# The tile of x1 serves once as a page for weights, then collects the experts' sums; x1 is added from its two parts later

## The chip, the cores and the metric

The kernel runs on 1 core of a Trainium2 chip. The metric is device time in microseconds (us) of one execution. Five engines work beside each other: PE (TensorE, matrix products; its weight loads are shown as PEld), DVE (VectorE), ACT (ScalarE), POOL (GpSimd) and SP (SyncE), which here does nothing but issue DMA transfers, in the order of the program. SBUF is the on-chip memory (128 partitions), PSUM the eight banks of 128 x 512 f32 into which PE writes.

## What is computed

One layer of an encoder on 256 tokens of width 2048, in f32. The part that matters here, cut from the reference:

```python
    x = x + merged @ w_out[i]                      # x1
    x = x + _hier_moe(_rmsnorm(x, g_ffn[i]), ...)  # 32 experts, top 2 of one group
    gate_p = jax.nn.sigmoid(_rmsnorm(x, g_ple[i]) @ w_ple_gate[i] + b_ple_gate[i])
    x = x + gate_p * (p[i] @ w_ple_up[i])
return _rmsnorm(x, g_final)
...
        hid = jax.nn.silu(xb @ w_g[e]) * (xb @ w_u[e])
        return (hid @ w_d[e]) * wt[:, None].astype(xb.dtype)
```

Ahead of it stand two token mixers with dense projections. An expert has w_gate and w_up of 2048 x 512 and w_down of 512 x 2048, 12 MB in f32; all 32 are read.

## The kernel before, in words

**Tokens and layout.** The 256 tokens are two blocks b of 128 partitions. `X[b]` is 128 x 2048 f32 (8 KB a partition) and holds x; `evac_out` adds the output projection into it chunk by chunk (four chunks c of 512 columns, L673), which makes x1. From there on X is called X2 and collects the experts' results.

**Pages and the stream.** All large weights come as pages of 128 x 4096 f32 (2 MB), each in one DMA (two of 1 MB for some). Class `Stream` (L40 on) holds a list `todo` of the loads in the order in which they will be used, and a list of free pages. `add(page)` tells that a page has been read; `pump` then issues the next load of the list into it (L67). Since SP works in the order of the program, an issue that must wait for the readers of its page also holds up every issue behind it. `add_half` (L74) and `add` (L82) issue a page in two halves at the first pair of experts.

The ring of pages in the expert stage has four pages `page`, two `pageX` and two `pageR` (called passing), eight in all; two are taken out on the way (`KEEP`: one from pair 4 on, which becomes `hpage`, and one from pair 8 on, for a product of the last part), so that six are left. The tile `pagePT` holds the tokens sorted for the experts (`xT`) and joins the ring after the loop.

**Two parts.** f32 products that matter for accuracy are made from two fp32r parts, hi and lo, whose sum is the f32 number. `evac_out`'s `lay` lays x1 as such parts `XP[b]` with columns rearranged ("t (p k) -> t k p", a step of 16 numbers, 64 bytes): hi is a copy by ACT (L680), lo = x1 − hi is a subtraction by DVE (L684). For the last chunk, lo is subtracted by POOL (L682, the list `last_lo`), beside the routing.

**Routing.** After x1 is ready PE makes the router's logits (L714 to L724), then warm-up transposes `keep_warm` (L300, 38 of them, then 20) while DVE works through a chain of small operations (L766 to L807) that finds each token's two experts; PE waits for its result at L811. Then one-hot matrices are made (L874, L876) and `dispatch` (L887, L890) sorts tokens by products with `XP`.

**The loop over pairs of experts** (P = 0 to 15; i = 0 gate, 1 up; j = four quarters of the rows; two quarters share a page of each of two experts):
- `gate_up` (L909): f32 products, two experts side by side on PE's columns, 16 per quarter.
- `hidden_gate` (ACT, L916), `hidden_up` (DVE, L920), `hidden_t` (PE transposes L924, ACT copy L925).
- in the next pair: `down_early(P-1)` (L974), the split of its result into hi and lo (`split_y`: ACT L933, DVE L934), and `combine_early(P-1)` (L963), which brings rows back to tokens, with a DVE addition into X2 (L967).
- for P below 8 w_down takes four pages; from P = 8 on only a first part of 512 columns is done in the loop, one page, and the remaining columns come in the tail.
- in odd pairs `dispatch` sorts tokens for the next two. After P = 6 there is a branch for experts with more than 64 tokens (`tc.If`, L984/L985), which SP waits for too.

The loads stand in the list in this order for each pair: gate quarters 0 and 1 (two pages, one per expert), w_down of the pair before, gate quarters 2 and 3, up 0 and 1, up 2 and 3. At the end come w_down of pair 15, then the remaining columns of w_down of pairs 8 to 10 (one page each, called i0, i1, i2), one page of `w_ple_gate`, i3, i4 and so on.

At P = 15 `st.retiring = True` takes both `pageR` out of the ring as they come free: their pool `rt2`, which holds `XP` too, is released after the loop, and the tail's tiles (`fin`, with the accumulators `ACC`) lie there.

**The tail** does the remaining products of w_down (L974), combines them (L1117, `add_rows` into X2), makes the gated term with three fp32r products (L1138 to L1140) and the final norm.

```python
 78      def add(self, *pages):
...
 85              if passing and self.retiring:
 86                  continue
```

Of the kernel before, what the change touches and what calls it, by code (L numbers as in the profile page):

```python
# [7 lines left out]
F32 = mybir.dt.float32  # L8
# [15 lines left out]
NL = NP - FULL  # L24
PPLE = 9
WARM = 12, 4
ROUTE_WARM = 38, 20
PARTS = ([(i, 2 * h + j) for h in range(2) for i in range(2) for j in range(2)],
         [(i, j) for i in range(2) for j in range(4)])
KEEP = {(4, 0, 1): 1, (8, 0, 1): 1}  # L30
# [9 lines left out]
class Stream:  # L40


    def __init__(self, nc):
        self.nc = nc
        self.free = deque()
        self.todo = deque()
        self.ready = deque()
        self.wanted = 0
        self.kept = deque()
        self.passing = []  # L50
        self.second = []
        self.retiring = False

    def want(self, *parts):

# [22 lines left out]
    def add(self, *pages):  # L78

        for page in pages:  # L80
            if self.second and page is self.second[0][0]:
                self.nc.sync.dma_start(page[:, 2048:4096], self.second.pop(0)[1][:, 2048:4096])  # L82
                continue
            passing = any(page is q for q in self.passing)
            if passing and self.retiring:
                continue
            if self.wanted and not passing:
                self.wanted -= 1
                self.kept.append(page)
            else:  # L90
                self.free.append(page)
        self.pump()
# [46 lines left out]
def body(tc, x, p, g_mix, w_in, w_pool, pool_scale, w_branch_a, sgu_ln_g, sgu_ln_b, w_spatial,  # L139
# [14 lines left out]
    psum = tc.alloc_tile_pool(name="psum", bufs=1, space=bass.MemoryType.PSUM)  # L154
    PS = [psum.tile([128, 512], F32, name=f"ps{i}") for i in range(8)]
    cst = tc.alloc_tile_pool(name="cst", bufs=1, side="left")
    cst.tile([128, 8], F32, name="gap0")
    base = tc.alloc_tile_pool(name="base", bufs=1, side="left")
    X = [base.tile([128, 2048], F32, name=f"x{b}") for b in range(2)]
    pg_pt = base.tile([128, 4096], F32, name="pagePT")  # L160
    pages = [base.tile([128, 4096], F32, name=f"page{i}") for i in range(4)]
    pg_pm, pg_t = pg_pt[:, 0:2048], pg_pt[:, 2048:4096]
# [438 lines left out]
                                       op=OP.mult)  # L601


    more = None
    MT, XP, yh, yl = [], [], [], []
    SG = [[pg_t[:, (2 * i + b) * 512:(2 * i + b + 1) * 512] for b in range(2)] for i in range(2)]

# [25 lines left out]
    for c in range(4):  # L633
        for i in range(2):
            unit(hT, evac_gate(c, i))
        if c == 0:
            drain()
            wk.release()
            mg = tc.alloc_tile_pool(name="mg", bufs=1, side="left", reuse_waits="tile")
            MT.extend(mg.tile([128, 512], F32R, name=f"mT{k}") for k in range(16))  # L640
            st.add(pages[3])
        if c == 1:
            bg.append(wr_gain)
        unit(zT, evac_y(c, 0))
        if c == 3:
            last_y = evac_y(c, 1)

            def end_y(banks):
                nonlocal rt, more
                todo = last_y(banks)  # L650
                rt.release()
                more = tc.alloc_tile_pool(name="more", bufs=1, side="right", reuse_waits="tile")
                rt = tc.alloc_tile_pool(name="rt2", bufs=1, side="right", reuse_waits="tile")
                st.passing = [rt.tile([128, 4096], F32, name=f"pageR{i}") for i in range(2)]
                XP.extend([rt.tile([128, 2048], F32R, name=f"x{n}{i}") for n in "hl"] for i in range(2))
                yh.extend(more.tile([128, 512], F32R, name=f"yh{i}") for i in range(2))
                yl.extend(more.tile([128, 512], F32R, name=f"yl{i}") for i in range(2))
                st.add(*st.passing)
                return todo

            unit(gT, end_y)
        else:
            unit(gT, evac_y(c, 1))
# [5 lines left out]
    def evac_out(c):  # L669
# [6 lines left out]
        def lay(b):  # L676

            hi, lo = (t.rearrange("t (k p) -> t k p", k=16)[:, :, 32 * c:32 * c + 32] for t in XP[b])
            src = X[b][:, cs].rearrange("t (p k) -> t k p", k=16)
            S_.activation(hi, src, AF.Copy)  # L680
            if c == 3:
                last_lo.append(lambda: P_.tensor_tensor(lo, src, hi.bitcast(F32), op=OP.subtract))  # L682
            else:
                V_.tensor_tensor(lo, src, hi.bitcast(F32), op=OP.subtract)  # L684

# [67 lines left out]
    oce = [ex.tile([128, T], F32R, name=f"oce{i}") for i in range(2)]  # L753
    hTe = [ex.tile([128, 4, 128], F32, name=f"hTe{i}") for i in range(2)]
    st.add(*[ex.tile([128, 4096], F32, name=f"pageX{i}") for i in range(2)])
    iot = ex.tile([128, 4, CAP], F32, name="iot")
    P_.iota(iot, pattern=[[WIN, 4], [1, CAP]], base=0, channel_multiplier=0, allow_small_or_imprecise_dtypes=True)
    rw = [hid[:, i * 64:(i + 1) * 64].rearrange("p (a e) -> p a e", a=8) for i in range(6)]
    ms1 = sm("ms1", [128, 2])
    vsum(ms1, ss1)  # L760
    r1 = inv_rms(ms1, "r1")
    for f in last_lo:
        f()
    L = sm("L", [128, 2, 36])
    for b in range(2):
        V_.scalar_tensor_tensor(L[:, b, :], lg[:, b, :], r1[:, b:b + 1], rb,  # L766
# [1 line left out]
    dbg("x1", X)  # L768
    dbg("L", [L])

    keep_warm(ROUTE_WARM[0], PS[4])

    Lg = L[:, :, 0:4]
# [184 lines left out]
    def combine_early(P, h):  # L958
        for c in ((2 * h, 2 * h + 1) if P < FULL else (0,) if not h else ()):
            banks = YE[0:2] if c % 2 else (T0, T1)  # L960
            for b in range(2):
                for y in (yh, yl):
                    mm(banks[b], oce[P % 2][:, b * 128:b * 128 + 128], y[c % 2], start=(y is yh), stop=(y is yl),  # L963
                       skip_group_check=True)
            for b in range(2):
                cs = slice(c * 512, (c + 1) * 512)
                V_.tensor_tensor(X2[b][:, cs], X2[b][:, cs], banks[b], op=OP.add)  # L967
        if not h and P < FULL:
            for c in range(2, 4):
                split_y(c % 2, YE[c], 512)  # L970
# [52 lines left out]
    def p_up():  # L1023
# [14 lines left out]
                S_.activation(pp[b][:, n * 512:(n + 1) * 512], (C0, C1)[b], AF.Copy)  # L1038
        st.add(page)

    onehots(lambda i, b: SW[:, i, b:b + 1])
    dispatch(xT, 0)
    dispatch(xT, 1)
# [3 lines left out]
    for P in range(NP):  # L1047
# [4 lines left out]
            pp = [page[:, b * D:(b + 1) * D] for b in range(2)]  # L1052
            p_up()
        if P == NP - 1:
            st.retiring = True
        for i, j in PARTS[bool(P)]:
            acc = accs[i]
            if not j % 2:
# [16 lines left out]
            if P == 0:  # L1075
                if (i, j) in ((0, 1), (1, 0)):
                    dispatch(xT, 2 + i)
                if (i, j) == (1, 1):
                    ci = late_routing()
            elif P % 2 and P < NP - 1 and i:  # L1080
                if j == 0:
                    onehots(lambda i, b: SQ[:, i, b, P // 2 + 1:P // 2 + 2])
                dispatch(xT, j)
            if (i, j) == (0, 2):
                slot_weights(pid[:, P:P + 1], wsl[:, P:P + 1])
                slot_scales(pid[:, P:P + 1], rsl[:, P:P + 1])
# [10 lines left out]
    down_early(NP - 1)  # L1097


    rt.release()  # L1100
    fin = tc.alloc_tile_pool(name="fin", bufs=1, side="right", reuse_waits="tile")
    oc2 = [fin.tile([128, 2 * T], F32R, name=f"oc{i}") for i in range(NL // 2)]
    oc = [oc2[i // 2][:, i % 2 * T:(i % 2 + 1) * T] for i in range(NL)]
    lx = [fin.tile([128, 512], F32R, name=f"lx{i}") for i in range(4)]
    flow = Flow(nc, fin, bg, look=2)
    gxs = [[fin.tile([128, 512], F32R, name=f"gx{i}{k}") for k in range(4)] for i in range(2)]
    gx, gx_idle = gxs[1], gxs[0]
    st.add(pg_pt)
    S_.activation(wsl[:, 0:1], wsl[:, 0:1], AF.Sigmoid)
    ACC = [fin.tile([128, 2048], F32, name=f"acc{b}") for b in range(2)]  # L1110
    ss2, ss3 = sm("ss2", [128, 2, 5]), ss0
    SPANS = ((0, EC),) + CHUNKS

# [212 lines left out]
```

## Time and profile before

| | us |
|---|---|
| median of 3 runs (1621.5 to 1624.71) | 1623.43 |
| the profiled execution | 1622.31 |
| its span in the profile | 1620.5 |

The granted TensorE clock is 0.979 in the mean. Busy time and share of the span:

| engine | us | share |
|---|---|---|
| PE | 1519.7 | 94% |
| PE weight loads | 879.0 | 54% |
| DVE | 633.8 | 39% |
| ACT | 422.6 | 26% |
| POOL | 26.6 | 2% |

DMA moves 526.64 MB, 325 GB/s in the mean. The expert stage runs from about 552 us (first L887) to about 1384 us, the tail from there.

In a timeline each row is start, duration, engine, line, operation, out<-in and the number of instructions that the row groups; in square brackets stands how long the engine was idle before it and what ended that. Rows with `SPq` are the issuing of DMA transfers by SP: a long one is a group with waits inside. A row of stretches has start:end, length, busy time and number of instructions of PE, PEld, DVE, ACT and POOL, then the granted clock, the mean busy share of the 16 DMA engines, and GB/s. A row of grouped instructions has busy time in us and the mean in ns of one, then the idle time before them and what ended it.

### The profile page before, as it was taken

What the parts mean: (1) busy time and instruction counts of PE and PEld (TensorE: products, weight loads), DVE (VectorE), ACT (ScalarE), POOL (GpSimd) and SP (SyncE); (2) the same over time, 40 slices, a digit from 0 to 9 for tenths busy, and PEclk for the clock granted to TensorE, in tenths of its full rate; (3) what the DMA queues carried; (4) which work ended last, traced back from release to release, by engine and by line L of the source; (5) the groups of instructions that cost most, each with busy time, mean ns of one, the idle gap of its engine ahead of it and who ended that gap; (6) DMA issues with size and microseconds to landing.
All of it is one profiled execution on the core that took longest, in us unless ns stands there. A gap on an engine that the chain in (4) does not pass through costs nothing. (4 is left out here: it accounts for less than half of the span.)

```text
span 1620.5 us, 17459 instructions
## 1 busy us (share of the span) xinstructions
PE 1519.7 (94%) x7009; PEld 879.0 (54%) x7009; DVE 633.8 (39%) x1119; ACT 422.6 (26%) x746; POOL 26.6 (2%) x38
## 2 busy tenths in 40 slices
PE   8999999999999999989979879999897987999994
PEld 6788888888888734324324324334242422456663
DVE  5764565656566414204213203212120211333457
ACT  4644454454455210100000000010000000332234
POOL 0000000000000100000000000000000000000004
PEclk9999999999999999999999989999999998999997
DMA  9656675555564699999999999999999999999881
GB/s 331 222 162 162 210 238 184 191 188 184 194 248 175 248 382 427 429 427 426 427 427 426 427 383 427 425 422 421 422 421 422 422 422 369 391 365 314 280 304 53
DMA packets 133096, 526.64 MB, mean 325 GB/s; under 512 B 16720, under 2 KB 43664, under 8 KB 110992
## 3 DMA queue, kind: packets, MB, share of 16 engines
q1 hardware_dynamic: 119184, 520.12, 82.1%
q10 hardware_dynamic: 13824, 5.34, 1.3%
q8 instruction: 57, 0.93, 0.2%
q14 instruction: 31, 0.25, 0.0%
HBM read 523.33 MB, written 2.10 MB: 324 GB/s over the span
## 5 line engine op out<-in xcount | busy, mean ns | idle before, releaser
L909 PE MATMUL ps<-page,pagePT 128*64 128x512 f32 x912 | 339.9, 609 | 11.9 <-DMA page<-in_w_exp_gate_dram 8.6
L121 DVE TENSOR_TENSOR wlo<-page,whi 128x512 fp32r<-128x512 f32 x358 | 246.6, 692 | 195.2 <-ACT whi L120 189.7
L120 ACT ACTIVATE whi<-page 128x512 fp32r<-128x512 f32 x358 | 224.7, 631 | 240.3 <-PE ps L394 207.1
L909 PE MATMUL ps<-pageX,pagePT 128*64 128x512 f32 x576 | 208.8, 622 | 24.3 <-DMA pageX<-in_w_exp_gate_dram 13.1
L909 PE MATMUL ps<-pageR,pagePT 128*64 128x512 f32 x560 | 189.3, 617 | 17.1 <-DMA pageR<-in_w_exp_gate_dram 10.8
L392 PE MATMUL ps<-whi,hT 128*128 128x512 f32 x448 | 184.3, 411 | 1.5 <-ACT whi L120 1.5
L934 DVE TENSOR_TENSOR yl<-ps,yh 128x512 fp32r<-128x512 f32 (+2 forms) x72 | 44.7, 630 | 344.8 <-ACT yh L933 344.8
L393 PE MATMUL ps<-wlo,hT 128*128 128x512 f32 x448 | 178.9, 399 | 0.4 <-DVE wlo L121 0.4
L394 PE MATMUL ps<-whi,hT 128*128 128x512 f32 x448 | 178.5, 399 | 0.0
L909 PEld LDWEIGHTS ps<-page,pagePT 128*64 128x64 f32 x912 | 96.9, 139 | 148.3 <-issue 125.5
L933 ACT ACTIVATE yh<-ps 128x512 fp32r<-128x512 f32 (+2 forms) x72 | 39.6, 549 | 361.6 <-PE ps L974 293.2
L909 PEld LDWEIGHTS ps<-pageX,pagePT 128*64 128x64 f32 x576 | 62.7, 142 | 113.8 <-issue 76.5
L909 PEld LDWEIGHTS ps<-pageR,pagePT 128*64 128x64 f32 x560 | 54.4, 141 | 84.2 <-issue 65.1
L392 PEld LDWEIGHTS ps<-whi,hT 128*128 128x128 f32 x448 | 85.2, 190 | 20.4 <-ACT whi L120 2.0
L394 PEld LDWEIGHTS ps<-whi,hT 128*128 128x128 f32 x448 | 85.0, 190 | 20.6
L393 PEld LDWEIGHTS ps<-wlo,hT 128*128 128x128 f32 x448 | 85.3, 190 | 19.4 <-DVE wlo L121 1.0
L890 DVE TENSOR_TENSOR pagePT<-ps,gfp 128x512 f32<-128x512 f32 x64 | 44.3, 692 | 130.8 <-PE ps L887 130.8
L967 DVE TENSOR_TENSOR x<-x,ps 128x512 f32<-128x512 f32 x80 | 50.0, 683 | 99.3 <-PE ps L963 99.3
L920 DVE SCALAR_TENSOR_TENSOR hid<-hid,wsl,ps 128x512 f32<-128x512 f32 x16 | 17.6, 1103 | 150.0 <-PE ps L909 149.2
L887 PE MATMUL ps<-OHd,xh 128*128 128x256 f32 x256 | 65.7, 295 | 0.0
L974 PE MATMUL ps<-page,hTe 128*64 128x512 f32 x224 | 59.8, 610 | 2.7 <-DMA page<-in_w_exp_down_dram 2.7
L887 PE MATMUL ps<-OHd,xl 128*128 128x256 f32 x256 | 62.1, 280 | 0.0
(271 smaller groups left out, 1842.9 us busy)
## 6 DMA issues: line engine op xcount, KB each, us to landing
page<-in_w_exp_gate_dram SPq DMA_DIRECT2D x32, 2048.0 KB, 19.8
page<-in_w_exp_up_dram SPq DMA_DIRECT2D x23, 2048.0 KB, 21.4
pageX<-in_w_exp_up_dram SPq DMA_DIRECT2D x21, 2048.0 KB, 20.0
pageR<-in_w_exp_up_dram SPq DMA_DIRECT2D x20, 2048.0 KB, 21.0
page<-in_w_merge_gate_dram SPq DMA_DIRECT2D x32, 1024.0 KB, 5.7
pageX<-in_w_exp_gate_dram SPq DMA_DIRECT2D x15, 2048.0 KB, 18.2
pageR<-in_w_exp_gate_dram SPq DMA_DIRECT2D x15, 2048.0 KB, 21.1
page<-in_w_exp_down_dram SPq DMA_DIRECT2D x14, 2048.0 KB, 23.6
```

Source lines behind the costliest of these rows:

```text
L120: nc.scalar.activation(hi, src, AF.Copy)
L121: nc.vector.tensor_tensor(lo, src, hi.bitcast(F32), op=OP.subtract)
L392: mm(banks[b], ah, hi, start=(k == 0), stop=False, skip_group_check=True)
L393: mm(banks[b], ah, lo, start=False, stop=False, skip_group_check=True)
L394: mm(banks[b], al, hi, start=False, stop=(k == nk - 1), skip_group_check=True)
L887: mm(ps[:, kk, :], XP[b][part][:, at:at + 128], OHd[:, b, 0:n], start=(not b and not part), stop=bool(b and part), skip_group_check=True)
L890: V_.tensor_tensor(xT[j][:, 2 * h:2 * h + 2, 0:n], ps, gfp[:, k0:k0 + 2, None].to_broadcast([128, 2, n]), op=OP.mult)
L909: mm(acc[i * 64:i * 64 + 64, :], xT[k // 4][:, k % 4, at + i * CAP:at + (i + 1) * CAP], ws[i], start=(k == 0), stop=(k == 15), skip_group_ ...
L933: S_.activation(yh[i][:, 0:w], y[:, 0:w], AF.Copy)
L934: V_.tensor_tensor(yl[i][:, 0:w], y[:, 0:w], yh[i][:, 0:w].bitcast(F32), op=OP.subtract)
L967: V_.tensor_tensor(X2[b][:, cs], X2[b][:, cs], banks[b], op=OP.add)
L974: mm(y[i * 64:i * 64 + 64, :], ht[:, k, i * 64:i * 64 + 64], ws[i], start=(k == 0), stop=(k == 3), skip_group_check=True)
```

## The change

1. X[0] and X[1] become the halves of one tile `pageS`, as large as a page. When x1's parts are laid, `pageS` is given to the stream for one load (`st.once`: a page in this list is not refilled). It takes the ninth load of the expert stage, the first gate page of P = 1. Then X2 lies in it: the first sums (of P = 0) are copied there by ACT instead of being added by DVE, and at P = 14 `add_x1` adds x1's hi and lo, sixteen DVE additions of 128 x 512, at a step of 64 bytes in X2.
2. The lo part of the last chunk is made by PE instead of POOL: identity x x1 (f32) plus negated identity x hi (fp32r) into PSUM, and a copy by ACT. The first warm-up has 20 transposes instead of 38. DVE makes the negated identity `nident` ahead of the routing chain.
3. `retiring` goes. At P = 15 only the first `pageR` leaves the ring; the second stays until the end of the loop, and holds `ACC` in the tail. `XP` gets a pool of its own, which the tail's other tiles take over.
4. `gap0` grows from 8 to 32 columns, which shifts the left side's tiles by 96 bytes.

```diff
-ROUTE_WARM = 38, 20
+ROUTE_WARM = 20, 20
...
         self.passing = []
+        self.once = []
         self.second = []
-        self.retiring = False
...
+            if any(page is q for q in self.once):
+                continue
             passing = any(page is q for q in self.passing)
-            if passing and self.retiring:
-                continue
...
-    cst.tile([128, 8], F32, name="gap0")
+    cst.tile([128, 32], F32, name="gap0")
     base = tc.alloc_tile_pool(name="base", bufs=1, side="left")
-    X = [base.tile([128, 2048], F32, name=f"x{b}") for b in range(2)]
+    pg_x = base.tile([128, 4096], F32, name="pageS")
+    X = [pg_x[:, b * 2048:(b + 1) * 2048] for b in range(2)]
...
                 more = tc.alloc_tile_pool(name="more", bufs=1, side="right", reuse_waits="tile")
+                xp = tc.alloc_tile_pool(name="xp", bufs=1, side="right", reuse_waits="tile")
                 rt = tc.alloc_tile_pool(name="rt2", bufs=1, side="right", reuse_waits="tile")
-                st.passing = [rt.tile([128, 4096], F32, name=f"pageR{i}") for i in range(2)]
-                XP.extend([rt.tile([128, 2048], F32R, name=f"x{n}{i}") for n in "hl"] for i in range(2))
+                XP.extend([xp.tile([128, 2048], F32R, name=f"x{n}{i}") for n in "hl"] for i in range(2))
+                st.passing = [(rt, more)[i].tile([128, 4096], F32, name=f"pageR{i}") for i in range(2)]
...
             if c == 3:
-                last_lo.append(lambda: P_.tensor_tensor(lo, src, hi.bitcast(F32), op=OP.subtract))
+                last_lo.append((b, lo, hi))
...
+    nident = ex.tile([128, 128], F32R, name="nident")
...
-    for f in last_lo:
-        f()
...
+    V_.tensor_scalar(nident, ident, -1.0, None, op0=OP.mult)
+    for b, lo, hi in last_lo:
+        ps = PS[3 + 2 * b].rearrange("t (k p) -> t k p", k=16)
+        mm(ps, ident, X[b][:, 1536:2048].rearrange("t (p k) -> t k p", k=16), start=True, stop=False, skip_group_check=True)
+        mm(ps, nident, hi, start=False, stop=True, skip_group_check=True)
+        S_.activation(lo, ps, AF.Copy)
+    st.add(pg_x)
+    st.once.append(pg_x)
     keep_warm(ROUTE_WARM[0], PS[4])
...
-                V_.tensor_tensor(X2[b][:, cs], X2[b][:, cs], banks[b], op=OP.add)
+                if P:
+                    V_.tensor_tensor(X2[b][:, cs], X2[b][:, cs], banks[b], op=OP.add)
+                else:
+                    S_.activation(X2[b][:, cs], banks[b], AF.Copy)
...
+    def add_x1(c):
+
+        for b in range(2):
+            o = X2[b][:, c * 512:(c + 1) * 512].rearrange("t (p k) -> t k p", k=16)
+            for part in XP[b]:
+                V_.tensor_tensor(o, o, part.rearrange("t (k p) -> t k p", k=16)[:, :, 32 * c:32 * c + 32].bitcast(F32), op=OP.add)
...
         if P == NP - 1:
-            st.retiring = True
+            st.once.append(st.passing[0])
...
+            if P == NP - 2 and i:
+                add_x1(j)
...
+    st.once.append(st.passing[1])
     rt.release()
+    xp.release()
     fin = tc.alloc_tile_pool(name="fin", bufs=1, side="right", reuse_waits="tile")
...
-    ACC = [fin.tile([128, 2048], F32, name=f"acc{b}") for b in range(2)]
+    ACC = [st.passing[1][:, b * 2048:(b + 1) * 2048] for b in range(2)]
```

On SP, at the start of the expert stage, these issues followed each other before (the last page of P = 0's gate, its last two of w_up, then the halves with which P = 0's first pages are refilled; the number at a tile's name tells it from its like):

```order
L67 DMA page_80<-in_w_exp_gate_dram 128x4096
L67 DMA pageX_3679<-in_w_exp_up_dram 128x4096
L67 DMA pageX_3680<-in_w_exp_up_dram 128x4096
L74 DMA page_78<-in_w_exp_gate_dram 128x2048
L74 DMA page_81<-in_w_exp_gate_dram 128x2048
L82 DMA page_78<-in_w_exp_gate_dram 128x2048
```

And now:

```order
L67 DMA pageX_3681<-in_w_exp_up_dram 128x4096
L67 DMA pageX_3682<-in_w_exp_up_dram 128x4096
L67 DMA pageS<-in_w_exp_gate_dram 128x4096
L74 DMA page_77<-in_w_exp_gate_dram 128x2048
L74 DMA page_80<-in_w_exp_down_dram 128x2048
L82 DMA page_77<-in_w_exp_gate_dram 128x2048
L82 DMA page_80<-in_w_exp_down_dram 128x2048
```

A whole page, `pageS`, stands ahead of the first half page and takes the first gate page of P = 1; the halves start one load further on, the second of them with w_down.

On SP in the last pair (from the last gate pages of P = 15 on), before:

```order
L67 DMA page_80<-in_w_exp_gate_dram 128x4096
L67 DMA pageX_3679<-in_w_exp_gate_dram 128x4096
L67 DMA pageX_3680<-in_w_exp_up_dram 128x4096
L67 DMA page_81<-in_w_exp_up_dram 128x4096
L67 DMA page_80<-in_w_exp_up_dram 128x4096
L67 DMA pageX_3679<-in_w_exp_up_dram 128x4096
L67 DMA pageX_3680<-in_w_exp_down_dram 128x4x512 x2
L67 DMA page_81<-in_w_exp_down_dram 128x4x512 x2
L67 DMA page_80<-in_w_exp_down_dram 128x4x512 x2
L67 DMA pageX_3679<-in_w_exp_down_dram 128x4x512 x2
L67 DMA pageX_3680<-in_w_ple_gate_dram 128x4x1024
L67 DMA pagePT<-in_w_exp_down_dram 128x4x512 x2
```

And now:

```order
L67 DMA page_78<-in_w_exp_gate_dram 128x4096
L67 DMA page_79<-in_w_exp_gate_dram 128x4096
L67 DMA pageX_3681<-in_w_exp_up_dram 128x4096
L67 DMA page_77<-in_w_exp_up_dram 128x4096
L67 DMA pageR_3020<-in_w_exp_up_dram 128x4096
L67 DMA page_78<-in_w_exp_up_dram 128x4096
L67 DMA page_79<-in_w_exp_down_dram 128x4x512 x2
L67 DMA pageX_3681<-in_w_exp_down_dram 128x4x512 x2
L67 DMA page_77<-in_w_exp_down_dram 128x4x512 x2
L67 DMA pageR_3020<-in_w_exp_down_dram 128x4x512 x2
L67 DMA page_78<-in_w_ple_gate_dram 128x4x1024
L67 DMA page_79<-in_w_exp_down_dram 128x4x512 x2
```

The third page of w_up goes into the second `pageR`, which held w_down of pair 14; before, it went into the page of the third gate page, which PE reads later. i3 goes into the page that w_down of pair 15 had, where it went into `pagePT`.

On PE between the router's logits and the first product of routing (`tri` is a triangular matrix, `O` the one-hot choice), before:

```order
L714 MATMUL ps_60<-ident,x_75 128x128 x4
L714 MATMUL ps_66<-ident,x_76 128x128 x4
L724 MATMUL ps_67<-wr,pagePT 128x36 x8
L300 MATMUL ps_64<-ident 128x128 x38
L811 LDWEIGHTS tri
L811 MATMUL ps_66<-O,tri 128x32
```

And now:

```order
L716 MATMUL ps_60<-ident,pageS 128x128 x4
L716 MATMUL ps_66<-ident,pageS 128x128 x4
L726 MATMUL ps_67<-wr,pagePT 128x36 x8
L776 MATMUL ps_63<-pageS,ident 128x512
L777 MATMUL ps_63<-xh_3015,nident 128x512
L776 MATMUL ps_65<-pageS,ident 128x512
L777 MATMUL ps_65<-xh_3017,nident 128x512
L301 MATMUL ps_64<-ident 128x128 x20
L821 LDWEIGHTS tri
L821 MATMUL ps_66<-O,tri 128x32
```

Four products stand ahead of the warm-up transposes, and eighteen of these are gone.

More of the change, by code (lines that the diff above doesn't have):

```diff
@@ L601, in body @@
                                        op=OP.mult)
-    more = None
+    more = xp = None
     MT, XP, yh, yl = [], [], [], []
@@ L648, in end_y @@
             def end_y(banks):
-                nonlocal rt, more
+                nonlocal rt, more, xp
                 todo = last_y(banks)
@@ L1097, in body @@
     down_early(NP - 1)
+    st.once.append(st.passing[1])
     rt.release()
+    xp.release()
     fin = tc.alloc_tile_pool(name="fin", bufs=1, side="right", reuse_waits="tile")
+    lx = [fin.tile([128, 512], F32R, name=f"lx{i}") for i in range(4)]
+    gxs = [[fin.tile([128, 512], F32R, name=f"gx{i}{k}") for k in range(4)] for i in (1, 0)][::-1]
     oc2 = [fin.tile([128, 2 * T], F32R, name=f"oc{i}") for i in range(NL // 2)]
     oc = [oc2[i // 2][:, i % 2 * T:(i % 2 + 1) * T] for i in range(NL)]
-    lx = [fin.tile([128, 512], F32R, name=f"lx{i}") for i in range(4)]
     flow = Flow(nc, fin, bg, look=2)
-    gxs = [[fin.tile([128, 512], F32R, name=f"gx{i}{k}") for k in range(4)] for i in range(2)]
     gx, gx_idle = gxs[1], gxs[0]
```

## The prediction

> **What bounds the kernel now.** I read the 40 slices of the page first, then busy time by stretches, then the timelines of PE and of the DMA-issuing queue where a stretch ends.
>
> ```profile
> span 1620.5 us, 17459 instructions
> DMA  9656675555564699999999999999999999999881
> 553.00:560.00 7.00, 7.00 (x45) 4.42 (x46) 2.77 (x4) 0.00 (x0) 0.00 (x0) 1.00 0.09 36
> 560.00:582.00 22.00, 22.00 (x126) 11.02 (x124) 6.82 (x27) 3.06 (x6) 0.00 (x0) 1.00 0.95 380
> 582.00:586.00 4.00, 4.00 (x22) 1.32 (x20) 0.00 (x0) 1.16 (x1) 0.00 (x0) 1.00 0.32 78
> 586.00:940.00 354.00, 325.28 (x1498) 131.61 (x1496) 87.82 (x159) 25.68 (x37) 0.00 (x0) 0.98 1.01 427
> 960.00:1340.00 380.00, 351.61 (x1584) 139.33 (x1580) 80.71 (x154) 26.02 (x36) 0.00 (x0) 0.98 1.01 423
> 1350.00:1356.00 6.00, 6.00 (x29) 2.69 (x29) 2.88 (x7) 1.15 (x1) 0.00 (x0) 1.00 0.48 158
> 1440.00:1580.00 140.00, 138.94 (x737) 89.27 (x736) 64.57 (x109) 47.02 (x99) 0.00 (x0) 1.00 0.89 305
> ```
>
> The last three numbers of a stretch are the granted clock, the DMA share and GB/s. From 586 us to 1340 the DMA engines are full (share 1.01, 427 and 423 GB/s) while PE idles for 354 − 325 = 29 us and 380 − 352 = 28 us: the experts' weights arrive as fast as they can, and the stage ends when the last byte does. Before that lie two holes in the stream: 553 to 560 (share 0.09) and 582 to 586 (0.32). A third is at 1350 to 1356 (0.48), in the last pair of experts. From 1440 PE is busy 138.94 of 140 us, so the tail is PE's and starts when its weights allow. A byte that moves from the full stretch into a hole is therefore time saved, at 427 GB/s.
>
> The first hole: the queue that issues the loads has no free page.
>
> ```profile
> 540.35 0.81 SPq L67 DMA_DIRECT2D pageX<-in_w_exp_up_dram  x2
> 559.92 0.80 SPq L74 DMA_DIRECT2D page<-in_w_exp_gate_dram  x2
> ...
> 584.22 0.80 SPq L67 DMA_DIRECT2D page<-in_w_exp_down_dram  x2
> ...
> 598.69 0.80 SPq L67 DMA_DIRECT2D page<-in_w_exp_up_dram  x2
> ...
> 695.84 3.65 PE L909 MATMUL ps<-page,pagePT 128*64 128x512 f32 x14 [2.17 <-DMA page<-in_w_exp_gate_dram]
> 1336.84 3.60 PE L974 MATMUL ps<-pageR,page 128*64 128x512 f32 x16
> 1337.03 17.50 SPq L67 DMA_DIRECT2D page<-in_w_exp_up_dram  x2
> 1361.45 1.07 PE L909 MATMUL ps<-page,pagePT 128*64 128x512 f32 x2 [0.19 <-DMA page<-in_w_exp_up_dram]
> 1344.38 1.11 PE L909 MATMUL ps<-pageX,pagePT 128*64 128x512 f32 x1 [3.10 <-DMA pageX<-in_w_exp_gate_dram]
> ```
>
> The eighth page is issued at 540.35 + 0.8, the ninth at 559.92, when PE has read the first half of a page. The second hole ends with the issues at 584.22, again a release by PE. PE first waits for a weight at 695.84; from there it follows the DMA. The third hole: in the group that starts at 1337.03 and lasts 17.50 us, the second issue comes at the group's end, 1354.2, because two pages have left the ring and the next one is being read.
>
> **The change, part by part.** The sum is made against the profiled execution, 1622.31 us (span 1620.5 and 1.81 around it); it stands 1.12 below the median 1623.43.
>
> *The page of x1 (pageS).* It adds one 2 MB load ahead of the ninth issue. It waits for the last readers of x1, PE's new products (below: two f32 ones from 543.8, so near 546), and queues behind the eighth and goes into the hole: 128 x 4096 x 4 bytes = 2.097 MB, at 427 GB/s 4.91 us, and the hole has (1 − 0.09) x 7 = 6.4 us. Every later load moves up by one place, while the releases by PE that open the second hole stay where they are: that hole keeps its size, one load further on. When the page has been read, at 598.69, one load is issued instead of two, since it is not refilled; the four loads issued from 584.22 to 598 take 4 x 4.91 = 19.6 us from there, so the DMA does not run dry. From there load k waits for the same release as before, with 4.9 us of head start. It survives to 1340, since the share is 1.01 all the way, and PE follows earlier data once it waits at all, from about 695. **Term: −4.9 us** (0 if the page comes too late, −4.9 at most, as the load is only 2 MB).
>
> *The lo part of the last chunk, now by PE.*
>
> ```profile
> 544.52 0.86 DVE L779 COPY hid<-L 128x64 f32<-128x64 f32 x1
> 545.67 1.22 DVE L782 TENSOR_TENSOR hid<-hid,m 128x64 f32<-128x64 f32 x1
> 547.44 0.23 DVE L782 TENSOR_TENSOR hid<-hid,f 128x64 f32<-128x64 f32 x1
> 549.52 0.23 DVE L807 TENSOR_TENSOR O<-hid 128x64 bf16<-128x64 f32 x1
> 543.80 3.02 POOL L682 TENSOR_TENSOR xl<-x,xh 128x512 fp32r<-128x512 f32 x2
> 541.98 1.98 PE L724 MATMUL ps<-wr,pagePT 128*128 128x36 f32 x16
> 543.79 4.35 PE L300 MATMUL ps<-ident 128*128 128x128 f32 x38
> 549.80 0.18 PE L811 MATMUL ps<-O,tri 128*128 128x32 bf16 x1 [1.66 <-DVE O L807]
> L1036 PE MATMUL ps<-pageX,page 128*128 128x512 f32 x32 | 14.0, 595 | 1.2 <-DVE page L1031 1.2
> 1405.22 0.23 PE ps L1139
> L680 ACT ACTIVATE xh<-x 128x512 fp32r<-128x512 f32 x8 | 8.6, 1092 | 0.0
> L925 ACT ACTIVATE page<-ps 128x512 f32<-128x512 f32 x8 | 4.8, 597 | 177.2 <-PE ps L924 177.2
> ```
>
> While POOL subtracts (543.80 to 546.82), two DVE operations of the routing chain take 0.86 and 1.22 us; one of the second's shape later takes 0.23. With POOL idle both fall to some 0.22: −1.6 us; the new negated identity (128 x 128) costs about 0.2 on the same chain. DVE is then ready at about 548.3 rather than 549.75.
>
> PE reaches this point at 543.8. It gets two full f32 products (two records each in L1036: 14.0/16 = 0.875 us), two fp32r ones (0.23, as L1139 takes for 512 columns in the chain of waits) and 20 warm-up transposes (4.35/38 = 0.114, so 2.29): 1.75 + 0.46 + 2.29 = 4.5, end 548.3, level with DVE. That is −1.4 at best. But the f32 product reads x1 with a step of 64 bytes. No row has a PE operand like that; the nearest are ACT, 1092 ns strided against 597 contiguous, and DVE below, 1057 against 682. With PE's f32 reads slowed by the same 1.8, PE ends 1.4 later, and with the fp32r ones too, at about 550.3, +0.6; with a factor of two +0.9. **I take −0.4**, between −1.4 and +0.9: a half-hidden cost, since f32 products already take 1.7 ns per column where ACT's strided element takes 2.1. [...] ACT's two copies (0.6 us each) take the place of nothing on the chain; its next work there comes after routing.
>
> *ACT instead of DVE for the first sums.* Eight copies at 0.6 us in P=1, beside PE that is busy all the time there: 0. If ACT were late, its split of the next y would be some 0.4 us later, before PE needs it.
>
> *x1 added late.* Sixteen DVE additions in P=14.
>
> ```profile
> 1306.92 0.16 DVE L919 TENSOR_TENSOR wsl<-wsl,rsl 128x1 f32<-128x1 f32 x1
> 1328.24 1.09 DVE L920 SCALAR_TENSOR_TENSOR hid<-hid,wsl,ps 128x512 f32<-128x512 f32 x1 [21.17 <-PE ps L909]
> 1333.46 0.60 ACT L925 ACTIVATE page<-ps 128x512 f32<-128x512 f32 x1 [24.11 <-PE ps L924]
> L684 DVE TENSOR_TENSOR xl<-x,xh 128x512 fp32r<-128x512 f32 x6 | 6.3, 1057 | 0.9 <-ACT xh L680 0.9
> L967 DVE TENSOR_TENSOR x<-x,ps 128x512 f32<-128x512 f32 x80 | 50.0, 683 | 99.3 <-PE ps L963 99.3
> ```
>
> DVE idles there from 1307.1 to 1328.24, 21.2 us. At 1.06 to 1.10 us each (L684, strided in; L920, strided in and out) they take 17.0 to 17.6: hidden, with 3.6 to spare. Behind them on DVE stands L920, whose result PE transposes (four, some 0.5 us by L300) before L925 starts: it is wanted near 1332.9. So they cost nothing up to (1332.9 − 1.1 − 1307.1)/16 = 24.7/16 = 1.54 us each. **0.**
>
> *The end of the last pair.* One page of two leaves the ring, not both. The third of the four last loads of w_up then goes into pageR1 as soon as PE has read w_down of P=14 there (L974 at 1336.84), near 1340.4, instead of at 1354.2.
>
> ```profile
> 1354.63 11.72 DMA pageX<-in_w_exp_up_dram
> 1366.40 9.46 PE ps L909 x30
> 1383.25 16.92 DMA pagePT<-in_w_exp_down_dram
> 1400.21 3.65 PE ps L974 x14
> 1364.00:1372.00 8.00, 5.60 (x16) 1.77 (x18) 0.00 (x0) 0.00 (x0) 0.00 (x0) 0.57 1.00 374
> ```
>
> This is the chain of waits: the last w_up lands at 1366.35, PE needs 9.46 us at a granted clock of 0.57 (after its wait), and then waits for the page that lands at 1400.2. That page is queued behind everything, so it comes earlier by what the hole loses: (427 − 158) GB/s x 6 us = 1.61 MB, 3.8 us; counted by the gap between shares (a little of the hole spills beyond 1356) 4.1. I take **−4.05**. PE gains more at w_up (4 us, and some 2 of the slow clock: 14 records take 3.65 us at full clock, in the row of 1400.21), but then waits for the page of 1396. From there PE is busy to the end, so it is passed on. Bounds: −2.5 (the next issue late by as much as the hole is short) to −6 (the later waits go as well).
>
> *The 96 bytes and the moved pools* change the place of tiles, no instruction: 0. In the rows above PE takes 3.60 to 3.65 us for a group from page, pageR and pagePT alike, whatever their places.
>
> Sum: −4.9 − 0.4 − 4.05 = −9.35: 1622.31 − 9.35 = 1613.0; from the median 1614.0.
>
> **The rivals.**
> 1. *The end gain is swallowed.* The load that PE waits for at 1400.21 now goes into the page of P=15's w_down, not into pagePT; if that page comes free late, the load starts no earlier. Then −4.9 − 0.4 = −5.3: 1618.1. Against it: that page is read out by one group of L974, about 3.65 us, and PE starts on it 4 to 6 us earlier than before; the loads ahead of it keep the DMA busy meanwhile.
> 2. *pageS brings nothing*: its load is issued after 553 or delays the ninth. Then −4.05 − 0.4: 1619.0. Against it: x1's last reader ends before 547.
> 3. *Neither*: the stream's rate is set by something else than its start, and the page of x1 only shifts the holes (the one at 582 widening by what the first shrinks), while at the end the freed page is not read early enough. 1623, with −0.4 inside the noise. Against it: the queue holds more than one load at every issue quoted from 559.92 on.
> 4. *Slower: the additions of P=14.* Reading and writing at a step of 64 bytes, with two SBUF inputs, might take more than any DVE row here. From 1.54 us each PE is late at L924; at P=15 it has 3.10 + 0.19 + 3.88 us of waits to make up (the last from 1361.45 + 1.07 to 1366.40), and 9.35 of gain, so the point at which the change loses is (24.7 + 7.2 + 9.35)/16 = 2.6 us. At 3 us: 48 − 24.7 − 7.2 − 9.35 = +6.8, 1630. Against it: the strided rows stand at 1.06 to 1.10, and no DVE row of this size takes 2. [...]
> 5. *More*: all terms at their good ends, −1.4 − 4.9 − 6 = −12.3: 1611; a little beyond, 1609.
>
> **How the numbers follow.** Forecast 0.60, at 1611 to 1617; rival 1: 0.16; rival 2: 0.08; rival 3: 0.07; rival 4: 0.05; rival 5: 0.04. About 0.2% (3.2 us) is what a measurement of this kernel can tell from no change. Faster by more than that: forecast, 1, 2 and 5, less 0.03 for the ends of 1 and 2 that come near 1620: 0.85. Within: 0.10. Slower: 0.05. The range holds the forecast and rivals 1 and 2 and leaves out 3, 4 and the far end: 1610 to 1620.
>
> **What would show it.** In the profile after: the hole at 553 carries pageS and the whole stream to 1340 stands some 5 us earlier (the wait at L985 too); the two DVE rows under POOL fall to 0.22, and PE's f32 product takes 0.44 a record or, if the stride costs, more; PE at L811 near 549.4; sixteen DVE additions of about 1.1 us each, done before L920; the share at 1350 near 1, the third of the last loads of w_up issued near 1335 (1340 less 4.9) instead of 1354, and the granted clock near 1360 no longer 0.57; the tail unchanged in length. I am wrong if the hole at 582 swallows the first term, if the tail starts no earlier than 1395, or if an addition takes over 1.5 us.

## The result and the profile after

| | us |
|---|---|
| before, median of 4 runs (1621.5 to 1625.36) | 1624.07 |
| after, median of 4 runs (1602.29 to 1604.02) | 1603.32 |
| ratio of the runs, 95% interval | 0.9874 (0.9857 to 0.9891) |
| after, the profiled execution | 1602.29 |
| its span | 1600.5 |

The change takes 20.8 us off, over twice what was forecast (9.35, to 1614.0, range 1610 to 1620). The page of the profile after, and its stretches (start:end, length, busy time of PE, PEld, DVE, ACT, POOL, then clock, DMA share, GB/s), with the DMA row in 40 slices:

```profile
span 1600.5 us, 17448 instructions
DMA  9656675555655799999999999999999999998881
536.00:582.00 46.00, 46.00 (x266) 24.41 (x266) 14.36 (x50) 6.60 (x10) 0.00 (x0) 1.00 0.89 358
582.00:936.00 354.00, 328.22 (x1516) 129.86 (x1514) 82.08 (x151) 29.50 (x45) 0.00 (x0) 0.98 1.01 427
956.00:1330.00 374.00, 343.64 (x1562) 138.44 (x1560) 94.44 (x166) 25.44 (x35) 0.00 (x0) 0.98 1.01 423
1344.00:1350.00 6.00, 3.29 (x18) 0.92 (x16) 0.00 (x0) 0.00 (x0) 0.00 (x0) 1.00 1.00 384
1440.00:1570.00 130.00, 127.64 (x682) 82.43 (x679) 63.24 (x111) 41.58 (x91) 0.74 (x2) 1.00 0.80 276
```

The expert stage still runs at 427 and 423 GB/s, the hole near 1350 is gone (share 1.00), and the tail is PE's. To see where the 20 us come from, the same instruction is looked up in both profiles at several places. Timelines of the profile after, PE and DVE (L726 is the last group of the router's logits, L930 is `hidden_up`, here of P = 0, 3, 9 and 14; the last row is the wait for i3):

```profile
531.87 1.98 PE L726 MATMUL ps<-wr,pagePT 128*128 128x36 f32 x16
546.21 7.09 PE L919 MATMUL ps<-page,pagePT 128*64 128x512 f32 x32
581.15 1.12 DVE L930 SCALAR_TENSOR_TENSOR hid<-hid,wsl,ps 128x512 f32<-128x512 f32 x1 [10.83 <-PE ps L919]
745.08 1.12 DVE L930 SCALAR_TENSOR_TENSOR hid<-hid,wsl,ps 128x512 f32<-128x512 f32 x1
1094.92 1.13 DVE L930 SCALAR_TENSOR_TENSOR hid<-hid,wsl,ps 128x512 f32<-128x512 f32 x1
1310.62 1.08 DVE L930 SCALAR_TENSOR_TENSOR hid<-hid,wsl,ps 128x512 f32<-128x512 f32 x1 [3.35 <-PE ps L919]
1380.24 3.65 PE L987 MATMUL ps<-page,page 128*64 128x512 f32 x14 [1.64 <-DMA page<-in_w_exp_down_dram]
```

And of the profile before (the logits, P = 14 and i3 stand in the prediction: 541.98, 1328.24, 1400.21):

```profile
591.19 1.12 DVE L920 SCALAR_TENSOR_TENSOR hid<-hid,wsl,ps 128x512 f32<-128x512 f32 x1 [10.77 <-PE ps L909]
760.24 1.12 DVE L920 SCALAR_TENSOR_TENSOR hid<-hid,wsl,ps 128x512 f32<-128x512 f32 x1
1110.52 1.12 DVE L920 SCALAR_TENSOR_TENSOR hid<-hid,wsl,ps 128x512 f32<-128x512 f32 x1
```

The lead (how much earlier the same instruction stands in the changed kernel) is 10.1 us at the logits already, before anything of the change but the new places of tiles has come into play; 10.0 at P = 0; 15.2 at P = 3 and 15.6 at P = 9; 17.6 at P = 14; 20.0 at i3 and at the end. (From P = 3 to 14 it moves by some 1.5 us either way around 16, as waits fall differently.) So the dense stage gives 10, the first hole 5, the end about 4, and routing nothing. The dense stage, where the prediction looked for nothing, in both profiles: groups of instructions of PE from 200 to 360 us (busy us, mean ns), and the stretch 200:360 whole, before:

```profile
L393 PE MATMUL ps<-wlo,hT 128*128 128x512 f32 x151 | 59.8, 396 | 0.0
200.00:360.00 160.00, 160.00 (x695) 128.67 (x694) 97.24 (x149) 82.25 (x137) 0.00 (x0) 1.00 0.60 197
```

and after:

```profile
L394 PE MATMUL ps<-wlo,hT 128*128 128x512 f32 x147 | 57.2, 389 | 0.0
200.00:360.00 160.00, 160.00 (x715) 132.08 (x714) 100.36 (x153) 84.45 (x140) 0.00 (x0) 1.00 0.62 204
```

PE is busy throughout at a granted clock of 1.00 in both, and does 715 instructions, nearly all of them fp32r products, where it did 695. One fp32r product of 512 columns starts every 0.2268 us instead of 0.2339 (5.67 us for 25 and 7.72 us for 33 in the timelines near 300 us). The stage has (448 + 64 + 64) x 3 = 1728 such products with hT, zT and gT; 1728 x 0.0071 = 12.3 us at most, and 10 arrive; in its first 80 us PE also waits (busy 73.92 us of 80 before, 72.80 after).

### The profile page after: what moved, and what is told of

Read it like the earlier page. It is cut to its first block, busy times and chain, and to the rows that moved or that the text cites. A ratio compares the mean times of both kernels' runs of the same rounds, so it can differ in the third digit from the quotient of the medians.

```text
span 1600.5 us, 17448 instructions
## 1 busy us (share of the span) xinstructions
PE 1502.0 (94%) x6997; PEld 872.1 (54%) x6997; DVE 642.7 (40%) x1128; ACT 427.9 (27%) x756; POOL 23.7 (1%) x36
## 5 line engine op out<-in xcount | busy, mean ns | idle before, releaser
L919 PE MATMUL ps<-page,pagePT 128*64 128x512 f32 x1056 | 401.6, 609 | 22.4 <-DMA page<-in_w_exp_gate_dram 15.9
L121 DVE TENSOR_TENSOR wlo<-page,whi 128x512 fp32r<-128x512 f32 x370 | 254.6, 692 | 187.3 <-ACT whi L120 182.9
L120 ACT ACTIVATE whi<-page 128x512 fp32r<-128x512 f32 x370 | 231.8, 631 | 232.8 <-PE ps L395 114.6
L919 PE MATMUL ps<-pageR,pagePT 128*64 128x512 f32 x576 | 221.5, 604 | 18.3 <-DMA pageR<-in_w_exp_gate_dram 11.3
L919 PEld LDWEIGHTS ps<-page,pagePT 128*64 128x64 f32 x1056 | 117.7, 139 | 164.4 <-issue 125.8
L919 PE MATMUL ps<-pageX,pagePT 128*64 128x512 f32 x400 | 156.2, 609 | 12.1 <-DMA pageX<-in_w_exp_up_dram 8.4
L919 PEld LDWEIGHTS ps<-pageR,pagePT 128*64 128x64 f32 x576 | 63.5, 138 | 91.5 <-issue 71.0
L987 PE MATMUL ps<-page,hTe 128*64 128x512 f32 x240 | 100.9, 609 | 5.0 <-DMA page<-in_w_exp_down_dram 5.0
L919 PEld LDWEIGHTS ps<-pageX,pagePT 128*64 128x64 f32 x400 | 45.2, 140 | 79.6 <-issue 61.3
L978 DVE TENSOR_TENSOR pageS<-pageS,ps 128x512 f32<-128x512 f32 x72 | 45.0, 683 | 86.6 <-PE ps L973 86.6
L930 DVE SCALAR_TENSOR_TENSOR hid<-hid,wsl,ps 128x512 f32<-128x512 f32 x16 | 17.7, 1105 | 129.7 <-PE ps L919 129.0
```

The source lines that it names most:

```text
L120: nc.scalar.activation(hi, src, AF.Copy)
L121: nc.vector.tensor_tensor(lo, src, hi.bitcast(F32), op=OP.subtract)
L919: mm(acc[i * 64:i * 64 + 64, :], xT[k // 4][:, k % 4, at + i * CAP:at + (i + 1) * CAP], ws[i], start=(k == 0), stop=(k == 15), skip_group_ ...
L987: mm(y[i * 64:i * 64 + 64, :], ht[:, k, i * 64:i * 64 + 64], ws[i], start=(k == 0), stop=(k == 3), skip_group_check=True)
```

## The experiments

Each is the kernel before or the changed kernel with one edit. Times are medians, except that g16 to g96 and e11 are single runs, and "before" is the kernel before, run beside them on the same chip. Its medians there lie between 1621.59 and 1624.07 us (one single run: 1625.31), and the changed kernel was not run beside its variants; so a difference of 2 us or less between two variants is not settled by times.

**The 96 bytes alone, and all but them.** `e1_gap32` is before with

```diff
-    cst.tile([128, 8], F32, name="gap0")
+    cst.tile([128, 32], F32, name="gap0")
```

> Before with gap0 of 32 columns instead of 8, nothing else. Theory 1 (the place of a tile within its row of SBUF decides the pace of the dense fp32r products): the products with hT, zT and gT start every 0.2268 us instead of 0.2343, the last dense product ends near 530 us instead of 540, and the kernel takes some 1613.5 us. Theory 2 (the 10 us of the dense stage come from another part of the change, or differ between executions): pace 0.2343, 1623.5 us.

Measured: 1612.01 us against 1623.61, ratio 0.9928 (0.9911 to 0.9944), and 715 products from 200 to 360 us:

```profile
200.00:360.00 160.00, 160.00 (x715) 132.15 (x714) 99.94 (x153) 84.47 (x139) 0.00 (x0) 1.00 0.63 204
```

`e2_after_gap8` is the same edit undone in the changed kernel.

> The changed kernel with gap0 back at 8 columns. Theory 1: the dense stage takes 10 us more again, the rest of the change stays: 1613.5 us, which is also the forecast's own sum for the other three parts. Theory 2: 1603.5 us.

Measured: 1615.03 us, 0.9949 (0.9932 to 0.9965) of before, with 695 products:

```profile
200.00:360.00 160.00, 160.00 (x695) 128.59 (x695) 97.32 (x149) 82.13 (x136) 0.00 (x0) 1.00 0.60 197
```

So theory 1 holds both ways: the 96 bytes give 11.6 us (9 to 14 by the interval of the ratio; 10.0 between the two profiled spans), and the other three parts together 8.6 (6 to 11), where 9.35 had been worked out.

**What about the place matters.** The left side's tiles (x, the pages, whi, wlo, mT) stand 288 bytes beyond a multiple of 512 before, the right side's (hT, zT, gT, pageR) 384; after the change both stand at 384. `e3_right48` moves the right side down instead:

```diff
-    pad.tile([128, 24], F32, name="gap")
+    pad.tile([128, 48], F32, name="gap")
```

> Before with the gap of the right side at 48 columns instead of 24: hT, zT and gT move down by 96 bytes, to the same place within 64, 128, 256 and 512 bytes as the whi and wlo tiles, which stay at 32 beyond a multiple of 64. Theory 1a (the two operands of a product must stand alike): pace 0.2268, some 1613.5 us. Theory 1b (the moving operand must start at a multiple of 64 or 128 bytes): pace 0.2343, 1623.5 us.

Measured: 1613.45 us, 0.9932 (0.9916 to 0.9949), 715 products: both at 288 is as good as both at 384. Not the place of one tile counts, but the distance between two. `x3_flow96` moves whi and wlo alone (and mT above them):

```diff
     spl = tc.alloc_tile_pool(name="spl", bufs=1, side="left", reuse_waits="tile")
+    spl.tile([128, 24], F32, name="gap1")
     flow = Flow(nc, spl, bg)
```

> Before with 96 bytes ahead of the flow's tiles whi and wlo alone (and of what is laid above them, mT); pages, x, pagePT and the identity stay. If the two operands of the product have to stand alike: the dense products with hT, zT and gT start every 0.2268 us, some 1612.5 us. If it is the place of the pages or of what ACT and DVE read meanwhile: 0.2343, 1623.5 us.

Measured: 1612.57 us, 0.9934 (0.9917 to 0.9951), 714 products, though x and the pages stay at 288 and the identity does not move:

```profile
200.00:360.00 160.00, 160.00 (x714) 131.96 (x714) 99.63 (x152) 84.20 (x139) 0.00 (x0) 1.00 0.62 204
```

The pair is the product's own two operands: the weights that PE loads (hT, zT, gT) and the tile that streams past them (whi, wlo). Then four more distances, one run each, by gap0 in the kernel before: 16 columns (64 bytes), 24 (32), 64 (128) and 96 (256).

> Before with gap0 of 16 columns: the left side's tiles (whi, wlo) then stand 64 bytes from the place of hT, zT, gT modulo 128 and alike modulo 64. If likeness modulo 64 bytes is enough, the dense products start every 0.2268 us (kernel some 1612 us); if it has to be modulo 128 or more, 0.2343 or another slower pace (1623.5).

> Before with gap0 of 24 columns: whi and wlo stand 32 bytes from the place of hT, zT, gT, modulo 64 to 512. A distance of 96 and of 64 bytes cost the same pace (0.2343 and 0.2333 us). If any distance below 128 costs it: 0.233 to 0.2345 and some 1622 us; if the cost grows with the distance: between 0.2268 and 0.233.

> Before with gap0 of 64 columns: distance 128 bytes, alike modulo 128, unlike modulo 256 and 512. If likeness modulo 128 is enough: pace 0.2268 us, some 1612 us. If it must be modulo 256 or 512: 0.233 to 0.2345 us, some 1622 us.

> Before with gap0 of 96 columns: distance 256 bytes, alike modulo 256, unlike modulo 512. If likeness modulo 256 is enough: pace 0.2268 us; if modulo 512: 0.233 to 0.2345 us. If distance 128 was already without cost, so is this.

The stretch 200:360 of each, in the order g16, g24, g64, g96:

```profile
200.00:360.00 160.00, 160.00 (x697) 128.86 (x697) 96.98 (x148) 82.72 (x137) 0.00 (x0) 1.00 0.60 197
```

```profile
200.00:360.00 160.00, 160.00 (x698) 128.90 (x697) 97.39 (x149) 82.55 (x136) 0.00 (x0) 1.00 0.59 197
```

```profile
200.00:360.00 160.00, 160.00 (x700) 129.67 (x699) 97.33 (x149) 82.80 (x137) 0.00 (x0) 1.00 0.59 198
```

```profile
200.00:360.00 160.00, 160.00 (x715) 132.12 (x714) 99.97 (x153) 84.47 (x139) 0.00 (x0) 1.00 0.62 204
```

Distances of 32, 64, 96 and 128 bytes all cost the pace (698, 697, 695, 700 products), 0 and 256 do not (715). Times: 1620.34, 1620.32, 1611.07 and 1612.02 us, beside 1621.59 (g16) and 1625.31 (the others). g64 does not fit: its dense stage is slow, and yet it is as fast as g96. Its DMA rate differs. The expert stage's stretches of g96:

```profile
600.00:900.00 300.00, 280.25 (x1290) 115.74 (x1286) 77.41 (x140) 22.78 (x33) 0.00 (x0) 0.98 1.01 428
980.00:1300.00 320.00, 298.42 (x1356) 121.05 (x1354) 67.03 (x128) 23.05 (x32) 0.00 (x0) 0.98 1.01 423
```

and of g64, whose left-side pages (all but the two pageR) stand at a multiple of 512 bytes:

```profile
600.00:900.00 300.00, 282.86 (x1310) 114.00 (x1307) 76.34 (x138) 22.13 (x32) 0.00 (x0) 0.98 1.01 430
980.00:1300.00 320.00, 299.56 (x1364) 121.94 (x1363) 68.41 (x130) 23.02 (x32) 0.00 (x0) 0.98 1.01 427
```

The share is the same, the rate 2 to 4 GB/s higher. `x2_before512` puts both sides of the kernel before at multiples of 512:

```diff
-    cst.tile([128, 8], F32, name="gap0")
+    cst.tile([128, 64], F32, name="gap0")
...
-    pad.tile([128, 24], F32, name="gap")
+    pad.tile([128, 120], F32, name="gap")
```

> Before with both sides at multiples of 512 bytes (gap0 of 64 columns, the right side's gap of 120): distance 0, all pages at 0 modulo 512. If the two effects are apart: the dense stage gains its 10 us, and the DMA runs at 431 GB/s or more from 600 to 900 us and 427 or more from 980 to 1300 (6 of 8 pages stood so in g64, with 430 and 427), which takes another 7 to 10 us out of the expert stage: 1604 to 1607 us. If the DMA's rate in g64 was an accident of that execution: 428 and 423, 1612.5 us.

```profile
200.00:360.00 160.00, 160.00 (x714) 132.16 (x713) 100.14 (x153) 84.33 (x138) 0.00 (x0) 1.00 0.62 203
600.00:900.00 300.00, 282.90 (x1306) 115.12 (x1304) 81.96 (x150) 23.38 (x33) 0.00 (x0) 0.98 1.01 430
980.00:1300.00 320.00, 297.68 (x1344) 117.69 (x1340) 65.64 (x126) 23.00 (x32) 0.00 (x0) 0.98 1.01 428
```

Measured: 1602.67 us against 1623.79, 0.9880 (0.9865 to 0.9896). Both effects are there, apart from each other, and two gaps alone take as much off as the whole change: 21.1 us against e1's 11.6. Between the two profiled spans (1598.5 and e1's 1610.5) lie 12.0 us. Of these 2.5 stand at the logits already (529.74 us against 532.21); what they hang on is not shown. Of the 9.5 behind them the higher rate in the full stretches makes some 6.9, an estimate (427 to 430 GB/s over 354 us and 423 to 428 over 380).

**The three parts that were costed.** `e4_no_page` is the changed kernel without

```diff
-    st.add(pg_x)
-    st.once.append(pg_x)
```

> The changed kernel without the load into pageS; the rest of it, the late addition of x1 too, stays. If the load fills the hole of the DMA at the start of the experts: 4.9 to 5.5 us more than the changed kernel, 1608.5 us, and the hole at the start back to a share of 0.1 over some 7 us. If the stream's rate is set by something else (rival 3 of the prediction): 1603.5 us.

Measured: 1608.81 us, 5.5 more than after (5.4 by the two ratios to before), with the first hole back:

```profile
536.00:582.00 46.00, 46.00 (x266) 24.55 (x265) 14.34 (x56) 6.71 (x10) 0.00 (x0) 1.00 0.77 310
543.00:550.00 7.00, 7.00 (x49) 4.82 (x49) 2.77 (x5) 0.00 (x0) 0.00 (x0) 1.00 0.18 75
```

Against 358 GB/s after, 46 us at 310 GB/s move 2.2 MB less: one page. `e5_both_retire` takes both pageR out of the ring again:

```diff
         if P == NP - 1:
-            st.once.append(st.passing[0])
+            st.once.extend(st.passing)
```

> The changed kernel with both pageR leaving the ring at P = 15, as before; the rest of the change stays. If the page that stays closes the hole of the DMA in the last pair: some 4.1 us more than the changed kernel, 1607.4 us, a hole of about 6 us again before the last pages of w_up, and the granted clock below 1 there. If the end gain is swallowed (rival 1 of the prediction): 1603.3 us.

```profile
1335.00:1340.00 5.00, 4.45 (x20) 1.34 (x18) 0.95 (x5) 1.13 (x1) 0.00 (x0) 1.00 0.56 197
1350.00:1360.00 10.00, 8.69 (x32) 2.66 (x28) 1.82 (x3) 0.04 (x1) 0.00 (x0) 0.83 1.04 387
```

Measured: 1607.05 us, 3.7 more than after (5.0 by the ratios); the hole (0.56) and the lower clock (0.83) are back. `e6_pool_lo` gives the last lo part to POOL again, with 38 transposes (the diff of the change, point 2, undone).

> The changed kernel with the last chunk's lo part made by POOL and 38 warm-up transposes, as before. By the forecast 0.4 us more than the changed kernel, by the trace of the changed kernel (first product of routing 9.8 us after the last dense one, 9.65 before) 0.1 less: between 1603.2 and 1603.7, which the time can't tell; the two DVE operations under POOL's subtraction take 0.9 and 1.2 us again. If POOL's 3 us hold up pageS and the hole is filled less: up to 2 us more.

Measured: 1603.03 us, 0.3 less than after (0.8 more by the ratios): this part of the change is worth nothing that these runs can tell. DVE's two operations take 0.86 and 1.23 us again, as expected.

`e10_warm4` shortens the first warm-up of the changed kernel:

```diff
-ROUTE_WARM = 20, 20
+ROUTE_WARM = 4, 20
```

> The changed kernel with 4 warm-up transposes ahead of routing's first product instead of 20. In the changed kernel DVE's choice is ready at 537.97 us and PE gets there at 539.83, after the transposes. If PE is the bound there: some 1.7 us less, 1601.6 us, and the rest of the run moves up by it. If the DMA's start decides the expert stage, or the granted clock falls: 1603.3 us or more.

Measured: 1601.89 us (1601.43 to 1603.19), 1.4 less than after, with runs of both overlapping; by the ratios to before (0.9875 and 0.9874) the two are alike. In its profile P = 0's `hidden_up` comes at 579.86, 1.3 us earlier than after, but P = 3's at 745.28 as after (745.08): there the DMA decides (share 1.01 from 582 to 936 us after), and PE's earlier start has gained nothing. Whether any of the 1.4 is real stays open.

`e11_contig`, one run, asks why L777 is slow (below); with this edit hi's numbers are subtracted in another order, so the kernel's result is no longer x1's lo part:

```diff
-        mm(ps, nident, hi, start=False, stop=True, skip_group_check=True)
+        mm(PS[3 + 2 * b], nident, XP[b][0][:, 0:512], start=False, stop=True, skip_group_check=True)
```

> The changed kernel with the two fp32r products of the last chunk's lo part (L777) reading 512 numbers in a row of hi's tile instead of its 16 runs of 32; which numbers are subtracted changes with it. In the changed kernel each takes about 1.05 us (start to next start) instead of the 0.23 that other fp32r products of this size take. If the 16 runs cost it: 0.23, and the first product of routing comes up to 1.6 us earlier after the last dense one; if the kind of product or its place in a group with an f32 product costs it: 1.05 as before.

```profile
534.27 1.40 PE L777 MATMUL ps<-xh,nident 128*128 128x512 f32 x1
535.46 1.91 PE L776 MATMUL ps<-pageS,ident 128*128 128x512 f32 x2
536.38 1.36 PE L777 MATMUL ps<-xh,nident 128*128 128x512 f32 x1
537.58 2.34 PE L301 MATMUL ps<-ident 128*128 128x128 f32 x20
```

Start to next start is 1.19 and 1.20 us, no less than with the 16 runs, so these are not the cause. (The kernel took 1604.42 us.)

**A version that beats both.** `x1_best` is the changed kernel with the gaps of x2_before512; the negated identity no longer finds room, so the lo part is POOL's as in e6_pool_lo.

> The changed kernel with both sides at multiples of 512 bytes and, for want of room for the negated identity, with the last lo part by POOL and 38 warm-up transposes (as in e6_pool_lo, 1603.0 us). By both effects: 7 to 10 us less than e6_pool_lo, 1593 to 1596 us. If the DMA's rate does not hang on the pages' place: 1603 us.

```profile
600.00:900.00 300.00, 284.87 (x1318) 114.99 (x1316) 78.21 (x144) 27.14 (x41) 0.00 (x0) 0.98 1.01 431
980.00:1300.00 320.00, 298.24 (x1342) 117.43 (x1340) 80.09 (x139) 23.09 (x32) 0.00 (x0) 0.98 1.01 428
```

Measured: 1593.64 us, 0.9820 (0.9807 to 0.9834) of before, 9.4 less than e6_pool_lo.

## Why the prediction was wrong, step by step

**The step that failed** is "*The 96 bytes and the moved pools* change the place of tiles, no instruction: 0. In the rows above PE takes 3.60 to 3.65 us for a group from page, pageR and pagePT alike". The rows are right and say nothing of the case: they are f32 products, two of them side by side at 0.44 us a record (32 records in 7.09 us), in a stage that waits for the DMA. The fp32r products of the dense stage start every 0.23 us, PE is busy throughout from 200 to 360 us, and the 96 bytes changed the distance between their two operands from 96 to 0. The runs put 11.6 us in the place of that 0 (e1), and leave 8.6 for the rest (e2). The trace of before had a sign of it. Groups of PE over the whole execution; the operand mT stands on the same side as whi and wlo, at the same place modulo 512:

```profile
L393 PE MATMUL ps<-wlo,mT 128*128 128x512 f32 x128 | 49.9, 390 | 0.0
L393 PE MATMUL ps<-wlo,gT 128*128 128x512 f32 x64 | 25.4, 396 | 0.0
```

The same line with the same wlo takes 390 ns with mT and 396 with gT. These two rows alone do not say that the place is the cause; the experiments do. In all of them mT keeps the place of wlo, and its row stays at 389 or 390 (after, e1, e3, g16 to g96), while gT's goes from 396 to 389 where gT comes to stand alike (after, e1, e3).

**The first hole, −4.9:** right. pageS is issued at 537.65 and the stream runs one page ahead; e4 measures 5.5. The second hole kept its size or nearly so, one load on (by the DMA shares, 0.75 from 578 to 590 us before and 0.81 from 568 to 580 after, some 3.0 and 2.3 us without a load).

**Routing, −0.4:** small, as said, but by other terms. After's rows:

```profile
534.42 0.19 DVE L789 COPY hid<-L 128x64 f32<-128x64 f32 x1
534.90 0.23 DVE L792 TENSOR_TENSOR hid<-hid,m 128x64 f32<-128x64 f32 x1
537.74 0.23 DVE L817 TENSOR_TENSOR O<-hid 128x64 bf16<-128x64 f32 x1
533.68 1.94 PE L776 MATMUL ps<-pageS,ident 128*128 128x512 f32 x2
534.65 1.21 PE L777 MATMUL ps<-xh,nident 128*128 128x512 f32 x1
535.69 1.88 PE L776 MATMUL ps<-pageS,ident 128*128 128x512 f32 x2
536.58 1.24 PE L777 MATMUL ps<-xh,nident 128*128 128x512 f32 x1
539.83 0.18 PE L821 MATMUL ps<-O,tri 128*128 128x32 bf16 x1
```

DVE gained what was worked out: both operations under POOL fell to 0.19 and 0.23, and the choice is ready 1.9 us before PE. The f32 product with the step of 64 bytes takes 0.97 and 0.89 us, hardly more than 0.875: the factor of 1.8 was not needed. The term that was mis-sized is the other: L777, 1.05 us instead of 0.23, twice. So PE reaches L821 7.96 us after the logits' last group began, against 7.82 before: +0.1. (The prediction's own sum for strided reads was too high: 548.3 + 1.4 + 0.4 is 550.1, or +0.3, and a factor of two gives +0.7. That −0.4 came near +0.1 is luck: it was a middle between two bounds that both take L777 at 0.23 to 0.46 us.)

**x1 added late, 0:** right. The sixteen additions take 1.04 us each in the mean and end at 1307.2, 3.4 us before `hidden_up`. **ACT's first copies, 0:** right, 603 ns each.

**The end, −4.05:** right in the step that was named; e5 measures 3.7 (5.0 by the ratios), and the lead grows by 4.4 from P = 9 to i3, 2.4 of it behind P = 14. The third page of w_up is issued at 1326.10. By the chain of waits of after, PE's 30 products there take 7.09 us, at full clock (1.00 from 1348 to 1356), instead of 9.46, and PE then waits for i3 as said:

```profile
1336.85 11.13 DMA page<-in_w_exp_up_dram
1348.03 7.09 PE ps L919 x30
1363.42 16.78 DMA page<-in_w_exp_down_dram
1380.24 3.65 PE ps L987 x14
```

**The rivals** all fell: 1, 2 and 3 by e5 and e4, 4 by the additions' 1.04 us, and 5, whose good ends add up to 12.3, by the 8.6 that e2 leaves for these terms. None of them, nor the bounds, had a price for the place of a tile in the stage where PE is the bound, so the true time lay outside the range.

## What to carry to other kernels

Before costing a moved tile at nothing, compare the rows of one instruction shape over all pairs of tiles, in the stage where that engine is busy throughout: 390 beside 396 ns was there to be read, and 1728 products made 10 us of it. In this kernel it paid to have the weights and the streamed operand of an fp32r product 0 or 256 bytes apart modulo 512 (0.2268 us a product instead of 0.232 to 0.234), and the pages that the DMA fills at a multiple of 512 (427 to 428 GB/s instead of 422 to 423 from 980 to 1300 us); gap tiles of 256 and 480 bytes in a partition did both, at the price of that room. And an edit's parts are best measured one by one: of the four here one was worth nothing, and the smallest was worth most.

## What the runs showed of the hardware

- An fp32r product of 128 x 128 weights and 512 columns starts every 0.2268 us (after; 714 to 716 instructions of PE from 200 to 360 us in all of these runs) when the two operands' places in a partition's row differ by 0 or 256 bytes, and every 0.232 to 0.234 when they differ by 32, 64, 96 or 128 (0.234, 0.233, 0.234 and 0.232 in the timelines near 300 us of g24, g16, before and g64), at a granted clock of 1.00. Why is not shown.
- Loads of 2 MB into pages at a multiple of 512 bytes ran at 430 to 431 GB/s from 600 to 900 us and 427 to 428 from 980 to 1300 (g64, x2_before512, x1_best; in g64 six of the eight pages stood so), into pages 128 to 384 bytes beyond it at 427 to 428 and 422 to 423 (before, after, e1, e3, e6, g16, g24, g96, x3). The runs do not tell 256 from 512, since no page stood 256 beyond. Why is not shown.
- The fp32r product of the negated identity with hi takes 1.05 us (start to next start, after's L777), four to five times as long as others of its size (0.2268), also when it reads 512 numbers in a row (1.2, e11). It follows an f32 product in the same PSUM bank and group; whether that is the cause wasn't tried.
